# Prompt attention of a two-layer decoder step: the order of the gate's multiplications by 1/sum against the evictions of score pieces

## The chip, the cores and the metric

The kernel runs on one core of a Trainium2 chip. A core has four engines that compute, each with its own queue of instructions that it runs in order: TensorE (PE in the profile; PEld is its loading of the stationary operand), VectorE (DVE), ScalarE (ACT) and GpSimd (POOL). SyncE (SP) issues transfers. Engines wait for each other by semaphores. TensorE writes into PSUM, eight banks of 2 KB in each of 128 partitions; VectorE and ScalarE bring results from there into SBUF. The metric is the device time of one execution, in microseconds; smaller is better.

## The reference, cut to what matters

One step of a two-layer decoder: an mLSTM layer, then a layer of attention with learned forgetting, each followed by a SwiGLU block, for a prompt of 1024 tokens behind 16 meta tokens and for 64 sampled tokens. The change lies in the attention of the prompt. With `q`, `k` already normalised and `c` the running sum of the log-forget values, that is

```python
s = jnp.einsum('bhqd,bkhd->bhqk', qi, k)          # 16 heads of 64
s = s + ci[..., None] - ckT[:, :, None, :]
s = jnp.where(pos_k[None, :] <= pi[:, None], s, -jnp.inf)
p = jax.nn.softmax(s, axis=-1)
o = jnp.einsum('bhqk,bkhd->bqhd', p, v)
...
return (o * jax.nn.sigmoid(og)) @ w_out
```

The kernel takes the division by the softmax's sum out of `p`: it multiplies `o * sigmoid(og)` by 1/sum afterwards, which is the same number.

## The kernel before, in words

The sixteen heads are taken as eight pairs (`hp`); the two heads of a pair lie in the two halves of the partitions (`z` = 0, 1). The 1024 queries are eight blocks of 128 (`qb` = 1 to 8), and two blocks (`u` = 0, 1) make a group `g` of 256 queries. Groups are worked in the order 0, 3, 1, 2 (`QG`).

**Score pieces.** `scores` (L2571) makes the scores of one block piece by piece (`KSPLIT`: up to 512 keys in a piece, 14 pieces in a head pair). A piece is two PSUM tiles `sp`, one for each head; the pool holds three. TensorE fills both with six matmuls that alternate between them (L2596; the inputs are split into a high and a low half, so there are three products for each). VectorE then evicts z = 0 and z = 1, each with one or two instructions (L2600) that add the forget values or the mask and keep the running maximum, which is read out behind each (DVE_READ_ACCUMULATOR). After a block's last piece POOL computes the bias `nb` (L2613, L2614), and ScalarE takes the exponentials in place, with their sum (L2623).

**Units.** A group's probabilities are worked in units of two key blocks; the last unit of a group is its tail. `turn` (L2636) transposes the probabilities on TensorE into a tile `tp` of two PSUM banks (two such tiles), ScalarE copies them out (L2658); a tail has columns left in `tp`, at places 6 and 7 of each half. In a tail the last 16 keys go through places 6 and 7 of the second half and are copied by L2660; VectorE takes 1/sum (L2663), and POOL spreads it over 64 columns (`rx`, L2666). `prod` (L2668) multiplies the transposed probabilities with the values into the output tile `op` (one bank; L2683, L2687, L2691). In a tail it also ends the group:

- four *spreading transposes* (L2678) first turn `rx`, so that 1/sum lies over the queries: two into places 6 and 7 of the first half of `tp`, two into columns 256 to 383 of the output bank;
- behind the product, VectorE multiplies the gate `og` by the output (L2694, 256 columns) and then the result by the two halves of 1/sum (L2697 twice, 128 columns each), one from `tp`, one from the output bank;
- POOL splits the result into a high and a low half (L2705, L2706).

**The order** is written out by hand, for TensorE, VectorE, ScalarE and POOL alike (`manual_schedule`). The loop over units (L2748 on) emits: a score piece if one is due (`ahead`), the unit's `turn`, its exponentials, another score piece if one is due, then the `prod` of the unit before. Pieces run 9 ahead (`LEAD`) and come at 0.7 for each call; so the pattern is the same for each head pair, and in it every tail's `prod` stands right behind a score piece, except at the end, when pieces have run out.

Of the kernel before, what the change touches and what calls it, by code (L numbers as in the profile page):

```python
# [11 lines left out]
ALU = mybir.AluOpType  # L12
# [2443 lines left out]
def attend_prompt(self, ys, slots, both, w):  # L2456


    nc, tc = self.nc, self.tc
    with self.pool("ap", bufs=1) as sp, self.pool("ap2", bufs=2) as s2, self.pool("app", bufs=2, space=PSUM) as pp:  # L2460
# [107 lines left out]

        rows = {}

        def scores(hp, g):  # L2571
# [7 lines left out]
            for u in range(2):  # L2579
# [11 lines left out]
                for n in KSPLIT[qb]:  # L2591
                    ps = [pp.tile([P, 512], F32, name=f"sp{hp}_{qb}_{c}_{z}", tag="sp", bufs=3) for z in range(2)]
                    for y, (a, b) in enumerate(((qh, kh), (qh, kl), (ql, kh))):
                        for z in range(2):
                            r = slice(z * 64, z * 64 + 64)
                            nc.tensor.matmul(ps[z][:, :n], a[r, qs], b[r, at : at + n], start=(y == 0), stop=(y == 2))  # L2596
                    parts = [(0, n)] if at + n < nk else [(0, n - P), (n - P, n)]
                    for z in range(2):
                        for y, (o, e) in enumerate(parts):
                            nc.vector.tensor_tensor_reduce(  # L2600
                                out=ss[z, u][:, at + o : at + e], in0=ps[z][:, o:e],
                                in1=diag[x][:, z] if y else ncb[:, z, at + o : at + e], scale=1.0,
                                scalar=mx[:, z, c + y - 1 : c + y] if c + y else NEG, op0=ALU.add, op1=ALU.max,
                                accum_out=mx[:, z, c + y : c + y + 1])
# [13 lines left out]
        def exps(n):  # L2618

            for _ in range(n):  # L2620
                _, _, ss, u, nb, sm = todo_exp.pop(0)
                for z in range(2):
                    nc.scalar.activation(ss[z, u], ss[z, u], AF.Exp, bias=nb[:, z : z + 1],  # L2623
                                         accum_out=sm[:, u, z : z + 1])

        def units(hp, g):


            vr, og = vals[hp]
# [5 lines left out]
            for j0 in range(0, nf, 2):  # L2635
# [3 lines left out]
                def turn(j0=j0, tail=tail, hold=hold):  # L2639
# [19 lines left out]
                    if tail:  # L2659
# [6 lines left out]
                        nc.gpsimd.tensor_copy(rx, hold["r"].unsqueeze(3).broadcast_to([P, 2, 2, DH]))  # L2666

                def prod(j0=j0, tail=tail, hold=hold):  # L2668
                    th = hold["th"]
                    mm = nc.tensor.matmul  # L2670
                    if tail:


                        hold["rs"] = [hold["pt"][:, 0, 6:], po[:, 256:384].rearrange("p (u q) -> p u q", u=2)]
                        for u in range(2):
                            for h, x in enumerate(hold["rs"]):
                                r = slice(h * 64, h * 64 + 64)
                                mm(x[:, u], hold["rx"][r, u].rearrange("p z d -> p (z d)"), self.ident[r, r],  # L2678
                                   start=(h == 0 or j0 == 0), stop=True, is_transpose=True, skip_group_check=True)
                    ds = [slice(z * 64, z * 64 + 64) for z in range(2)]  # L2680
# [13 lines left out]
                    nc.vector.tensor_tensor(out=y, in0=po[:, :256], in1=y, op=ALU.mult)  # L2694
                    for h, x in enumerate(hold["rs"]):
                        yh = y.rearrange("p (u h q) -> p h u q", u=2, h=2)[:, h]
                        nc.vector.tensor_tensor(out=yh, in0=x, in1=yh, op=ALU.mult)  # L2697
                    c0 = T0 + 256 * g
# [9 lines left out]

                out.append((turn, prod))
            return out  # L2710
# [12 lines left out]
        with tc.manual_schedule(engines={E.PE, E.DVE, E.Activation, E.Pool}):  # L2723
# [10 lines left out]
            def ahead(slot):  # L2734

                nonlocal made
                while made < ns and made < LEAD + slot * ns / (2 * nu):
                    next(todo, None)
                    made += 1
                    if slot == 0:  # L2740
                        for _ in range(2):
                            next(gate, None)
                        exps(len(todo_exp) - 1)

            late = None
            slot = 0
            todo_exp = []
            for hp, g in groups:  # L2748
                us = None
                for k in range(g + 1):  # L2750
# [14 lines left out]
                    us[k][0]()  # L2765
                    exps(n)
                    ahead(slot + 1)
                    if late:
                        late()
                    late = us[k][1]  # L2770
                    slot += 2
# [7 lines left out]
                if (hp, g) in groups[4:6]:  # L2779
                    next(tile0)  # L2780
            late()
    return ws
# [34 lines left out]
```

## Time and profile before

| what | value |
|---|---|
| median of 3 runs | 2872.78 us (2870.52 to 2873.95) |
| the profiled execution's own time | 2874.75 us |
| its span in the profile | 2873.1 us |
| prompt attention within the span | about 1791 to 2024 us |
| granted TensorE clock, mean | 0.997 |
| output product's multiplication, L2694 | 32 times, median 421 ns |
| multiplication by 1/sum, L2697 | 64 times, 280 to 293 ns |
| spreading transposes, L2678 | 128 times, median 220 ns |

A row of the timeline gives the start within the span, the time taken, the engine, the line, the operation, the tiles (result, arrow, inputs), the shape and how many instructions are merged; in brackets the idle time of that engine just before, and what ended it by the profile. For TensorE the ends of matmuls are modelled, and they overlap: a row's time is not what the engine is held for. Waits are listed as "who <- for whom: total, times, longest". Releasers are inferred: of several semaphores the last is named.

### The profile page before, as it was taken

What the parts mean: (1) busy time and instruction counts of PE and PEld (TensorE: products, weight loads), DVE (VectorE), ACT (ScalarE), POOL (GpSimd) and SP (SyncE); (2) the same over time, 40 slices, a digit from 0 to 9 for tenths busy, and PEclk for the clock granted to TensorE, in tenths of its full rate; (3) what the DMA queues carried; (4) which work ended last, traced back from release to release, by engine and by line L of the source; (5) the groups of instructions that cost most, each with busy time, mean ns of one, the idle gap of its engine ahead of it and who ended that gap; (6) DMA issues with size and microseconds to landing.
All of it is one profiled execution on the core that took longest, in us unless ns stands there. A gap on an engine that the chain in (4) does not pass through costs nothing.

```text
span 2873.1 us, 53648 instructions
## 1 busy us (share of the span) xinstructions
PE 2795.3 (97%) x20485; PEld 2674.7 (93%) x20485; DVE 1726.0 (60%) x3478; ACT 1310.9 (46%) x2622; POOL 1017.8 (35%) x1495
## 2 busy tenths in 40 slices
PE   7999989999999999999999999999999999999999
PEld 7998979999999999999999888677999999999999
DVE  6044555887777655553345444776478777765553
ACT  6122464444444434443444444777344444443432
POOL 3022333075556311115352102454307655531210
PEclk9999999999999999999999999999999999999999
DMA  7057656122222275544453676442413222237652
GB/s 214 16 144 170 164 159 182 49 88 78 79 84 78 98 264 197 203 150 136 139 174 123 238 279 220 143 148 85 158 48 94 75 75 84 78 98 255 219 184 101
DMA packets 312443, 400.19 MB, mean 139 GB/s; under 512 B 28142, under 2 KB 235050, under 8 KB 311162
## 3 DMA queue, kind: packets, MB, share of 16 engines
q1 hardware_dynamic: 277234, 277.79, 30.4%
q0 software_dynamic: 33728, 118.38, 12.6%
q8 instruction: 161, 2.64, 0.4%
q14 instruction: 96, 0.79, 0.1%
q10 hardware_dynamic: 1224, 0.60, 0.1%
HBM read 299.92 MB, written 96.77 MB: 138 GB/s over the span
## 4 chain that ended last, share of the span: by engine, by line
PE 69%; DVE 10%; issue 4%; ACT 3%; DMA 2%; POOL 1%; DVEq 0%; ACTq 0%; POOLq 0%; SPq 0%
PE m L1505 23%; PE dps L266 6%; PE dps L268 6%; PE dps L267 6%; PE tmps L266 3%; PE tmps L267 3%; PE tmps L268 3%; DVE slot L339 2%; PE sp L2596 1%; DVE s L2600 1%; PE op L2683 1%; PE pops L266 1%; PE pops L267 1%; PE pops L268 1%; PE bps L266 1%
## 5 line engine op out<-in xcount | busy, mean ns | idle before, releaser
L339 DVE TENSOR_TENSOR slot<-slot,slot 128x1024 fp32r<-128x1024 f32 (+3 forms) x263 | 266.5, 1016 | 133.9 <-ACT slot L338 125.4
L338 ACT CAST slot<-slot 128x1024 fp32r<-128x1024 f32 (+3 forms) x263 | 206.7, 788 | 236.3 <-PE dps L267 90.1
L1505 PE MATMUL m<-x1h,slot 128*128 128x384 f32 x640 | 178.3, 338 | 3.1 <-DVE ns L1481 1.5
L1505 PE MATMUL m<-x0h,slot 128*128 128x336 f32 x640 | 167.0, 316 | 0.0
L413 POOL TENSOR_TENSOR ns<-ns,nq 128x384 f32<-128x384 f32 (+1 forms) x59 | 63.8, 1081 | 210.9 <-ACT nq L411 209.7
L1505 PE MATMUL m<-x2h,slot 128*128 128x384 f32 x480 | 135.8, 337 | 0.0
L1612 POOL DMA_DIRECT2D hr<-hT x60 | 32.5, 542 | 281.6 <-DVE T_2l L339 68.8
L108 POOL TENSOR_TENSOR slot<-vA 128x256 f32<-128x256 f32 x80 | 74.9, 946 | 151.2 <-DMA vA<-in_w_gate_up 147.5
L108 POOL TENSOR_TENSOR slot<-Ht 128x256 f32<-128x256 f32 x80 | 74.9, 946 | 150.9 <-DMA Ht<-in_w_gate_up 147.2
L339 DVE TENSOR_TENSOR slot<-Ht,slot 128x256 fp32r<-128x256 f32 (+3 forms) x101 | 84.9, 842 | 63.6 <-ACT slot L338 63.6
L339 DVE TENSOR_TENSOR slot<-vA,slot 128x256 fp32r<-128x256 f32 (+3 forms) x101 | 85.5, 849 | 62.2 <-ACT slot L338 62.2
L1505 PEld LDWEIGHTS m<-x1h,slot 128*128 128x128 f32 x640 | 117.1, 188 | 4.4 <-DVE ns L1481 2.1
L1505 PEld LDWEIGHTS m<-x0h,slot 128*128 128x128 f32 x640 | 113.3, 188 | 0.0
L1505 PE MATMUL m<-x1l,slot 128*128 128x384 f32 x320 | 107.8, 337 | 0.0
L1505 PE MATMUL m<-x0l,slot 128*128 128x336 f32 x320 | 101.0, 316 | 0.0
L1505 PE MATMUL m<-T_2h,slot 128*128 128x384 f32 x320 | 96.8, 343 | 3.0 <-ACT Ht L1511 0.9
L2623 ACT ACTIVATE s<-s,nb 128x272 f32<-128x272 f32 (+7 forms) x126 | 98.9, 786 | 0.1
L2658 ACT COPY th<-tp 128x768 f32<-128x768 f32 (+1 forms) x80 | 73.4, 919 | 55.3 <-PE tp L2650 32.6
L1505 PE MATMUL m<-T_4h,slot 128*128 128x384 f32 x320 | 95.3, 338 | 0.0
L108 POOL TENSOR_TENSOR Ht<-Ht 128x512 f32<-128x512 f32 (+1 forms) x60 | 84.5, 1408 | 28.4 <-DVE wl1l L339 28.4
L108 POOL TENSOR_TENSOR vA<-vA 128x512 f32<-128x512 f32 (+1 forms) x60 | 84.4, 1408 | 27.5 <-DVE wl0l L339 27.5
L2029 DVE TENSOR_REDUCE ss<-sqb 128x4 f32<-128x256 f32 (+1 forms) x72 | 30.2, 419 | 102.8 <-ACT sqb L2028 102.0
(843 smaller groups left out, 10286.8 us busy)
## 6 DMA issues: line engine op xcount, KB each, us to landing
slot<-in_w_down SPq DMA_DIRECT2D x88, 512.0 KB, 4.4
wr<-in_w_down SPq DMA_DIRECT2D x42, 512.0 KB, 4.7
wraw<-in_w_in_a SPq DMA_DIRECT2D x40, 512.0 KB, 4.0
vA<-in_w_gate_up SPq DMA_DIRECT2D x40, 512.0 KB, 3.9
Ht<-in_w_gate_up SPq DMA_DIRECT2D x40, 512.0 KB, 4.1
hr<-hT POOLq DMA_DIRECT2D x46, 384.0 KB, 5.5
kp<-in_cache_k SPq DMA_DIRECT2D x32, 512.0 KB, 5.6
vp<-in_cache_v SPq DMA_DIRECT2D x32, 512.0 KB, 6.3
```

The source lines that it names most:

```text
L108: self.net.nc.gpsimd.tensor_tensor(out=o, in0=a, in1=b, op=op)
L266: mm(ps, sh, mh, start=first, stop=False)
L267: mm(ps, sh, ml, start=False, stop=False)
L268: mm(ps, sl, mh, start=False, stop=last)
L338: self.nc.scalar.copy(hi, src)
L339: self.nc.vector.tensor_tensor(out=lo, in0=src, in1=hi.bitcast(F32), op=ALU.subtract)
L413: (nc.vector if x >= late else nc.gpsimd).tensor_tensor(out=s, in0=s, in1=sq, op=ALU.add)
L1505: nc.tensor.matmul(u.b[b][:, :n], w[p][:, k], x[q][:, k], start=new and k == i == 0, stop=k == 1 and i == 2, skip_group_check=True)
L1612: nc.gpsimd.dma_start(hraw[j], hT[t][:, 2 * c : 2 * c + 2])
L2029: nc.vector.tensor_reduce(out=ss[:m, i, :], in_=sq[:m].rearrange("p (h d) -> p h d", d=DH), op=ALU.add, axis=AX.X)
L2623: nc.scalar.activation(ss[z, u], ss[z, u], AF.Exp, bias=nb[:, z : z + 1], accum_out=sm[:, u, z : z + 1])
L2658: nc.scalar.copy(th.rearrange("p x z (u h q) -> p h (x z u) q", h=2, q=64)[:, :, :n], pt[:, :, :n])
```

## The change

The part of `prod` that multiplies by 1/sum becomes two functions of its own. `spread` issues the four spreading transposes, now all into places 6 and 7 of the two halves of `tp`. `scale` issues the two multiplications of `og` by 1/sum, before `og` is multiplied by the output. The loop hands the pair to the next score piece: `scores` calls `spread` behind the piece's six matmuls, and `scale` between the eviction of z = 0 and that of z = 1. If no piece comes, `flush` calls both just ahead of `prod`. The multiplication by the output comes last.

```diff
--- before.py
+++ after.py
@@ -2567,6 +2567,7 @@
                                         in1=mask.unsqueeze(1).broadcast_to([P, 2, P]), op=ALU.add)
 
         rows = {}
+        between = []
 
         def scores(hp, g):
 
@@ -2595,7 +2596,12 @@
                             r = slice(z * 64, z * 64 + 64)
                             nc.tensor.matmul(ps[z][:, :n], a[r, qs], b[r, at : at + n], start=(y == 0), stop=(y == 2))
                     parts = [(0, n)] if at + n < nk else [(0, n - P), (n - P, n)]
+                    spread, scale = between.pop() if between else (None, None)
+                    if spread:
+                        spread()
                     for z in range(2):
+                        if z and scale:
+                            scale()
                         for y, (o, e) in enumerate(parts):
                             nc.vector.tensor_tensor_reduce(
                                 out=ss[z, u][:, at + o : at + e], in0=ps[z][:, o:e],
@@ -2665,18 +2671,22 @@
                             [P, 2, 2, DH], F32, name=f"rx{hp}_{g}", tag="rx")
                         nc.gpsimd.tensor_copy(rx, hold["r"].unsqueeze(3).broadcast_to([P, 2, 2, DH]))
 
+                def spread(j0=j0, hold=hold):
+                    hold["rs"] = [hold["pt"][:, h, 6:] for h in range(2)]
+                    for u in range(2):
+                        for h, x in enumerate(hold["rs"]):
+                            r = slice(h * 64, h * 64 + 64)
+                            nc.tensor.matmul(x[:, u], hold["rx"][r, u].rearrange("p z d -> p (z d)"), self.ident[r, r],
+                                             start=True, stop=True, is_transpose=True, skip_group_check=True)
+
+                def scale(hold=hold):
+                    for h, x in enumerate(hold["rs"]):
+                        yh = og[g].rearrange("p (u h q) -> p h u q", u=2, h=2)[:, h]
+                        nc.vector.tensor_tensor(out=yh, in0=x, in1=yh, op=ALU.mult)
+
                 def prod(j0=j0, tail=tail, hold=hold):
                     th = hold["th"]
                     mm = nc.tensor.matmul
-                    if tail:
-
-
-                        hold["rs"] = [hold["pt"][:, 0, 6:], po[:, 256:384].rearrange("p (u q) -> p u q", u=2)]
-                        for u in range(2):
-                            for h, x in enumerate(hold["rs"]):
-                                r = slice(h * 64, h * 64 + 64)
-                                mm(x[:, u], hold["rx"][r, u].rearrange("p z d -> p (z d)"), self.ident[r, r],
-                                   start=(h == 0 or j0 == 0), stop=True, is_transpose=True, skip_group_check=True)
                     ds = [slice(z * 64, z * 64 + 64) for z in range(2)]
                     for x in range(1 if tail else 2):
                         for z in range(2):
@@ -2692,9 +2702,6 @@
                                start=False, stop=(u == 1))
                     y = og[g]
                     nc.vector.tensor_tensor(out=y, in0=po[:, :256], in1=y, op=ALU.mult)
-                    for h, x in enumerate(hold["rs"]):
-                        yh = y.rearrange("p (u h q) -> p h u q", u=2, h=2)[:, h]
-                        nc.vector.tensor_tensor(out=yh, in0=x, in1=yh, op=ALU.mult)
                     c0 = T0 + 256 * g
                     for t, (t0, t1) in enumerate(TS):
                         a, b = max(c0, t0), min(c0 + 256, t1)
@@ -2706,7 +2713,7 @@
                             nc.gpsimd.tensor_tensor(out=xl[:, hp, xs], in0=ya, in1=xh[:, hp, xs].bitcast(F32),
                                                     op=ALU.subtract)
 
-                out.append((turn, prod))
+                out.append((turn, prod, (spread, scale) if tail else None))
             return out
 
         groups = [(hp, g) for hp in range(8) for g in QG]
@@ -2741,6 +2748,12 @@
                         for _ in range(2):
                             next(gate, None)
                         exps(len(todo_exp) - 1)
+
+            def flush():
+                for pair in between:
+                    for f in pair:
+                        f()
+                between.clear()
 
             late = None
             slot = 0
@@ -2764,10 +2777,13 @@
                         n = max(n - m, 0)
                     us[k][0]()
                     exps(n)
+                    if late and late[2]:
+                        between.append(late[2])
                     ahead(slot + 1)
                     if late:
-                        late()
-                    late = us[k][1]
+                        flush()
+                        late[1]()
+                    late = us[k]
                     slot += 2
                     if g == QG[1] and k == 2 and hp < 7:
                         load_v(hp + 1, nc.sync)
@@ -2778,7 +2794,9 @@
                         wo_split(k)
                 if (hp, g) in groups[4:6]:
                     next(tile0)
-            late()
+            for f in late[2]:
+                f()
+            late[1]()
     return ws
```

On VectorE, at the tail of group 2 (`og_2`), with the last piece of block 4 (`s_4_0`, `s_4_1`: z = 0 and 1) and the first of block 5, the order before was:

```order
L2600 ISA s_4_0_19364,mx_4_19366<-sp_4_1_0_19408,nd_4_19138,mx_4_19366 128x128
...
L2600 ISA s_4_1_19365,mx_4_19366<-sp_4_1_1_19409,ncb_18561,mx_4_19366 128x128
...
L2600 ISA s_4_1_19365,mx_4_19366<-sp_4_1_1_19409,nd_4_19138,mx_4_19366 128x128
...
L2694 TENSOR_TENSOR og_2_18599<-op_2_19228,og_2_18599 128x256
L2697 TENSOR_TENSOR og_2_18599<-tp_2_4_19336,og_2_18599 128x2x64
L2697 TENSOR_TENSOR og_2_18599<-op_2_19228,og_2_18599 128x2x64
L2600 ISA s_5_0_19446,mx_5_19448<-sp_5_0_0_19449,ncb_18561 128x400
```

and on the same engine at the same place after it:

```order
L2606 ISA s_4_0_19364,mx_4_19366<-sp_4_1_0_19408,nd_4_19138,mx_4_19366 128x128
...
L2685 TENSOR_TENSOR og_2_18599<-tp_2_4_19336,og_2_18599 128x2x64 x2
L2606 ISA s_4_1_19365,mx_4_19366<-sp_4_1_1_19409,ncb_18561,mx_4_19366 128x128
...
L2606 ISA s_4_1_19365,mx_4_19366<-sp_4_1_1_19409,nd_4_19138,mx_4_19366 128x128
...
L2704 TENSOR_TENSOR og_2_18599<-op_2_19228,og_2_18599 128x256
L2606 ISA s_5_0_19446,mx_5_19448<-sp_5_0_0_19449,ncb_18561 128x400
```

Both multiplications by 1/sum (now L2685) moved from behind the output product's to between the two evictions, and both read `tp`; L2704 is the former L2694.

On TensorE, at the tail of group 3 with the first piece of block 7, the order before was:

```order
L2596 MATMUL sp_7_0_0_20282<-kh_19702,ql_19704 128x512
L2596 MATMUL sp_7_0_1_20283<-kh_19702,ql_19704 128x512
L2678 MATMUL tp_3_6_20197<-ident,rx_3_20219 128x64
L2678 MATMUL op_3_20032<-ident,rx_3_20219 128x64
L2678 MATMUL tp_3_6_20197<-ident,rx_3_20219 128x64
L2678 MATMUL op_3_20032<-ident,rx_3_20219 128x64
L2683 MATMUL op_3_20032<-th_3_6_20198,vr_19591 64x256 x2
L2687 MATMUL op_3_20032<-th_3_6_20198,vr_19591 64x128 x2
L2691 MATMUL op_3_20032<-tail_18551,vr_19591 64x32 x4
L2596 MATMUL sp_7_1_0_20309<-kh_19702,qh_19701 128x400
```

and after it:

```order
L2597 MATMUL sp_7_0_0_20282<-kh_19702,ql_19704 128x512
L2597 MATMUL sp_7_0_1_20283<-kh_19702,ql_19704 128x512
L2679 MATMUL tp_3_6_20197<-ident,rx_3_20219 128x64 x4
L2693 MATMUL op_3_20032<-th_3_6_20198,vr_19591 64x256 x2
L2697 MATMUL op_3_20032<-th_3_6_20198,vr_19591 64x128 x2
L2701 MATMUL op_3_20032<-tail_18551,vr_19591 64x32 x4
L2597 MATMUL sp_7_1_0_20309<-kh_19702,qh_19701 128x400
```

Nothing moved on TensorE; only the target of two of the four spreading transposes (now L2679) is another.

## The prediction

> **What bounds the kernel now.** The shares by engine and the windows come first: they say which engine limits the stage that the change touches. The profiled run took 2874.75 us, 2.0 above the median of the runs shown (2872.78) and 1.7 above its own span; what is won or lost below is taken off the median.
>
> ```profile
> span 2873.1 us, 53648 instructions
> ...
> PE 2795.3 (97%) x20485; PEld 2674.7 (93%) x20485; DVE 1726.0 (60%) x3478; ACT 1310.9 (46%) x2622; POOL 1017.8 (35%) x1495
> ...
> 1791.00:2024.00 233.00, 216.54 (x3062) 162.32 (x3062) 162.58 (x783) 176.44 (x362) 111.82 (x291) 0.99 0.40 130
> 2023.00:2060.00 37.00, 37.00 (x234) 36.81 (x233) 15.00 (x22) 10.01 (x16) 14.64 (x20) 1.00 0.69 226
> ```
>
> Prompt attention lies in 1791 to 2024 us. The columns of the window are length, then busy time of PE, PEld, DVE, ACT, POOL. TensorE is busy 216.5 of 233 us, so all its visible idle time is 16.5 us, and the change cannot win more than about that. Behind the stage TensorE is busy without a gap (37.00 of 37.00), so what the stage wins is kept. Next come the waits of the stage (us in total, times, longest).
>
> ```profile
> DVE s L2600 <- PE sp L2596: 29.7, 29, 2.4
> ...
> DVE og L2694 <- PE op L2691: 8.1, 3, 4.6
> PE sp L2596 <- DVE mx L2600: 7.2, 17, 0.9
> ...
> PE tp L2650 <- DVE og L2697: 4.0, 7, 0.6
> ```
>
> VectorE waited for the output product only 3 times in 32 tails: elsewhere, when it reaches the product's multiplication, the product is there already. So VectorE idles ahead of a piece's first eviction (29.7 us), not between evictions and gate. TensorE in turn waits for evictions (7.2) and, once per head pair, for the gate multiplication that frees a transposes' tile (4.0). The timeline shows how these meet. The order of one head pair comes back every 28.9 us (1913.86 to 1942.75 under C), with the same four tails. I call them A (group 3, with the first piece of block 7), B (group 1, second piece of block 8), C (group 2, last piece of block 4 of the next pair), D (group 0, last piece of block 5).
>
> Place A:
>
> ```profile
> 1954.18 0.22 PE L2678 MATMUL tp<-ident,rx 64*128 64x64 f32 x1
> ...
> 1954.43 0.69 DVE L2600 CUSTOM_DVE_ANT_0 s<-sp,slot 128x512 f32<-128x512 f32 x1 [1.06 <-PE op L2678]
> ...
> 1955.05 0.69 DVE L2600 CUSTOM_DVE_ANT_0 s<-sp,slot 128x512 f32<-128x512 f32 x1
> ...
> 1955.66 0.42 DVE L2694 TENSOR_TENSOR og<-op,og 128x256 f32<-128x256 f32 x1
> ...
> 1956.18 0.29 DVE L2697 TENSOR_TENSOR og<-tp,og 128x128 f32<-128x128 f32 x1
> 1956.39 0.28 DVE L2697 TENSOR_TENSOR og<-op,og 128x128 f32<-128x128 f32 x1
> ...
> 1956.58 0.49 DVE L2600 CUSTOM_DVE_ANT_0 s<-sp,slot,mx 128x272 f32<-128x272 f32 x1
> ...
> 1957.73 0.76 PE L2596 MATMUL sp<-slot,slot 64*128 64x384 f32 x5 [0.52 <-DVE mx L2600]
> ```
>
> From 1954.43 VectorE runs without a gap: eviction z=0, eviction z=1, output product, two multiplications by 1/sum, next piece. At 1957.73 TensorE has waited 0.52 us for that next piece's z=0. The spreading transposes were done at 1954.40, long before the first eviction ended.
>
> Place C, with the row of the head pair before it first:
>
> ```profile
> 1913.86 0.71 PE L2650 MATMUL tp<-ident,s 64*128 64x64 f32 x16 [0.58 <-DVE og L2697]
> ...
> 1940.34 0.35 DVE L2600 CUSTOM_DVE_ANT_0 s<-sp,ncb,mx 128x128 f32<-128x128 f32 x1 [1.50 <-PE sp L2596]
> ...
> 1941.12 0.35 DVE L2600 CUSTOM_DVE_ANT_0 s<-sp,ncb,mx 128x128 f32<-128x128 f32 x1
> ...
> 1941.78 0.42 DVE L2694 TENSOR_TENSOR og<-op,og 128x256 f32<-128x256 f32 x1
> ...
> 1942.31 0.29 DVE L2697 TENSOR_TENSOR og<-tp,og 128x128 f32<-128x128 f32 x1
> ...
> 1942.71 0.56 DVE L2600 CUSTOM_DVE_ANT_0 s<-sp,ncb 128x400 f32<-128x400 f32 x1
> ...
> 1942.75 0.71 PE L2650 MATMUL tp<-ident,s 64*128 64x64 f32 x16 [0.58 <-DVE og L2697]
> ...
> 1943.20 0.08 DVE L2600 DVE_READ_ACCUMULATOR2_ANT mx<- 128x1 f32 x1
> ...
> 1943.24 0.49 PE L2596 MATMUL sp<-kh,qh 64*128 64x256 f32 x2
> ```
>
> Here the transposes of the next unit wait 0.58 us for the first multiplication by 1/sum. Places B and D, the waits for the output bank:
>
> ```profile
> 1933.02 0.42 DVE L2694 TENSOR_TENSOR og<-op,og 128x256 f32<-128x256 f32 x1
> ...
> 1933.39 0.66 PE L2650 MATMUL tp<-ident,s 64*128 64x64 f32 x16
> ...
> 1933.76 0.28 DVE L2697 TENSOR_TENSOR og<-op,og 128x128 f32<-128x128 f32 x1
> ...
> 1934.19 0.44 PE L2683 MATMUL op<-th,vr 128*64 128x256 f32 x2
> ...
> 1945.33 0.42 DVE L2694 TENSOR_TENSOR og<-op,og 128x256 f32<-128x256 f32 x1
> ...
> 1946.07 0.28 DVE L2697 TENSOR_TENSOR og<-op,og 128x128 f32<-128x128 f32 x1
> ...
> 1946.49 1.08 PE L2683 MATMUL op<-th,vr 128*64 128x256 f32 x8 [0.18 <-PE sp L2596]
> ```
>
> The next group's first product writes the bank that the second multiplication still reads: that one ends at 1933.76 + 0.28 = 1934.04 and at 1946.35, and the product starts 0.15 and 0.14 later. The row names "PE sp", but the order of starts says it is this release.
>
> **The change, part by part.** *Nothing is added or removed.* The four spreading transposes and the three multiplications of each of the 32 tails stay, with their sizes; on TensorE they keep their places behind the score matmuls and ahead of the product. Cost 0 there. The transposes now write only the probabilities' tile; they waited already for the copy of that tile's tail (ScalarE) and for the spread sums (POOL), and still do.
>
> *The burst on VectorE.* Before, from the output product to the next piece: 0.52 (1955.66 to 1956.18) + 0.21 + 0.19 = 0.92; at C 1941.78 to 1942.71, 0.93. The 0.52 holds a gap of 0.10 behind the product, because the multiplication reads what it wrote. Afterwards the two multiplications stand ahead of z=1 (0.21 + 0.19, they follow each other without a wait), and the product is followed by an eviction that does not need it. That pair is not in the trace. Bounds: at most the 0.52 as now, at least 0.34, which is 0.42 less the 0.08 by which the two multiplications overlap (0.29 long, 0.21 apart). I take 0.34 or 0.35, since a follower that reads nothing of it is nearest to that pair. The burst then takes 0.40 + 0.35 = 0.75, **0.17 shorter**. The bound from above is 0.
>
> *A* is then 0.17 shorter, 7 times (in the last head pair no piece is left at the last three tails): the wait of 0.52 shrinks to 0.35. It does not go, because VectorE has the same work between its first eviction and the next piece.
>
> *C.* The tile is free after the second multiplication, 1941.12 + 0.21 + 0.28 = 1941.61, so the wait of 0.58 goes. What is late next: the score piece behind those transposes needs the z=0 eviction that begins at 1942.71, read out at 1943.20. Before, the transposes' wait covered that; afterwards the read-out comes at 1943.03, and TensorE, there at about 1942.7, stands again until about 1943.16. The wait changes its name, and 0.17 is won, 7 times.
>
> *B and D.* The output bank is freed by the end of the product, which starts 0.40 later than now: at B 1933.02 + 0.40 + 0.42 = 1933.84 in place of 1934.04, 0.19 to 0.20 earlier. At B the transposes end at 1934.05 and products elsewhere start just as such a row ends, so TensorE can use it. 0.19 x 7 at B. D has a score piece in the first head pair too, 0.19 x 8.
>
> *The end.* In the last head pair nothing stands between:
>
> ```profile
> 2016.93 0.71 PE L2650 MATMUL tp<-ident,s 64*128 64x64 f32 x16
> 2017.05 0.43 DVE L2694 TENSOR_TENSOR og<-op,og 128x256 f32<-128x256 f32 x1 [0.25 <-PE op L2691]
> ...
> 2017.71 0.28 DVE L2697 TENSOR_TENSOR og<-op,og 128x128 f32<-128x128 f32 x1
> ...
> 2018.14 1.08 PE L2683 MATMUL op<-th,vr 128*64 128x256 f32 x8 [0.50 <-DVE r L2663]
> ```
>
> With both multiplications done beforehand the bank is free at 2017.05 + 0.43 = 2017.48, the transposes end at 2017.64: 0.5 is won, once.
>
> *What the move puts at risk.* The z=1 eviction ends 0.40 later in the tails. Behind it wait the bias on POOL, then the exponentials; at D:
>
> ```profile
> 1945.84 0.19 POOL L2614 TENSOR_TENSOR nb<-nb,cqP 128x2 f32<-128x2 f32 x1
> ...
> 1946.80 0.84 ACT L2623 ACTIVATE s<-s,nb 128x656 f32<-128x656 f32 x1
> ```
>
> The bias is there 0.77 before it is used, so 0.40 fits: 0. The piece two further on needs that buffer (at C from about 1942.4, wanted at 1942.7): 0.
>
> Sum: 7 x 0.17 + 7 x 0.19 + 7 x 0.17 + 8 x 0.19 + 0.5 = 1.2 + 1.3 + 1.2 + 1.5 + 0.5 = **5.7 us**, so 2872.8 - 5.7 = 2867.1. These waits lie one behind the other on the way TensorE, VectorE, TensorE, so they add.
>
> **Rivals.** *The gap stays whoever follows.* If the 0.52 behind the product stands with any follower, A and C win nothing; B, D and the end stay: 15 x 0.19 + 0.5 = 3.4, so 2869.4. The row for it is the 0.10 itself; against it, the two multiplications that start 0.21 apart although each lasts 0.28 or more. [...]
>
> *The waits go altogether.* If VectorE found time for the multiplications where it idles now, the waits of A, C and D would vanish: 7 x (0.52 + 0.58 + 0.19) + 8 x 0.18 + 0.5 = 11.0, so 2861.8. For it speaks the idle 1.06 and 1.50 ahead of the first evictions; against it, that the multiplications stand behind that first eviction, not in the gap.
>
> *It does not reach the end.* ScalarE is busy 176 of 233 us, and if its copies end the same waits, nothing is won: 2872.8. Against it: no row of A to D names ScalarE.
>
> *Slower.* If VectorE restarts with the 0.10 gap at each of the three new joints (first eviction to multiplication, multiplication to second eviction, that to product), the burst grows by 0.30 - 0.17 = 0.13 at A and C, and the release at B and D comes 0.30 - 0.19 = 0.11 later: 14 x 0.13 + 15 x 0.11 - 0.5 = 3.0, so 2875.8; with the wait for the transposes paid in each tail too (0.1 x 29) 2878.7. It decides from 0.6 us for the two multiplications in place of 0.40. Against it, the product now starts with the read-out of the eviction ahead of it, without a gap.
>
> **How the numbers follow.** 0.2% is 5.7 us, about what a measurement of this kernel can tell from no change. The forecast has 0.52 and lies on that bound; I put 0.33 of it beyond, as no small gain (a wait instruction less on TensorE in some tails) is in the sum, and 0.19 within. The staying gap has 0.13 and the unreached end 0.07, both within. The vanishing waits have 0.16, all faster. The slower case has 0.12: 0.07 beyond, 0.05 within. So faster 0.49, same 0.44, slower 0.07. The range runs from 2861.5 (waits gone) to 2874.5 (nothing won and the spread of the runs, 1.2 above the median); outside lie most of the slower case and some of the fastest, about 0.15. The likeliest case by itself has 2865 to 2869.
>
> **What would show it.** Right: the wait of the transposes for the gate (4.0, 7 times) is gone and the wait of score matmuls for evictions has grown at C to about 0.4 and fallen to about 0.35 at A; the output product is followed by an eviction 0.34 to 0.35 later; the head pair's period falls from 28.9 to about 28.2. Wrong: a gap at the new joints, the product still 0.52 ahead of its follower, an exponential that waits for the bias, or waits at A that vanish.

## The result: 7.75 us less, most of it found in prompt attention

The changed kernel takes 2862.77 us (median of 11 runs, 2856.89 to 2866.77), the kernel before 2870.52 us (median of 11 runs, 2866.90 to 2873.95). The ratio is 0.9977 with an interval of 0.9969 to 0.9985, that is 4.3 to 8.9 us faster. A second measurement gave 0.9978 (0.9969 to 0.9987). The forecast was 2867.1, or 5.7 less than before.

The profiled spans differ by more than the medians. Here is the head of the page of the changed kernel:

```profile
span 2855.2 us, 53625 instructions
...
PE 2790.4 (98%) x20485; PEld 2671.0 (94%) x20485; DVE 1724.8 (60%) x3478; ACT 1311.8 (46%) x2622; POOL 1018.3 (36%) x1495
```

Of the 17.9 us between the spans, 9.9 lie ahead of prompt attention: its first score matmul starts at 1773.41 before and at 1763.56 after, and nothing was changed ahead of it. So the stage has to be measured by itself. I take it from one instruction to another that both kernels have: the last output-gate product ahead of the first transposes (1791.18 before) to the first product of the output projection (2024.65 before). The columns are those of the window rows in the prediction. The kernel before, its first profile:

```profile
1791.18:2024.65 233.47, 217.01 (x3066) 162.79 (x3066) 163.05 (x783) 176.26 (x362) 112.29 (x291) 0.99 0.40 130
```

and a second one, taken later (before_again, below):

```profile
1784.50:2016.36 231.86, 215.49 (x3065) 162.05 (x3065) 162.95 (x782) 176.37 (x362) 112.30 (x291) 1.00 0.40 131
```

The changed kernel, its first profile:

```profile
1781.14:2006.41 225.27, 215.03 (x3066) 161.86 (x3065) 160.08 (x784) 176.92 (x362) 112.35 (x292) 1.00 0.41 134
```

and a second one (after_again, below):

```profile
1787.17:2012.42 225.25, 215.02 (x3065) 161.85 (x3065) 160.08 (x784) 176.93 (x362) 111.94 (x292) 1.00 0.40 134
```

The stage is 225.27 and 225.25 us long, before 233.47 and 231.86. The 1.6 between the two profiles of the kernel before is no work: it is TensorE's clock, in the first profile (the seventh number, PEclk):

```profile
1840.00:1842.00 2.00, 1.40 (x8) 0.92 (x9) 1.43 (x10) 0.74 (x2) 1.22 (x5) 0.67 0.57 209
1842.00:1844.00 2.00, 2.00 (x12) 0.86 (x14) 0.87 (x4) 0.00 (x0) 0.98 (x2) 0.50 0.18 58
```

So the change is worth 231.86 - 225.25 = **6.6 us** in the stage at full clock. It comes from TensorE's idle time, 231.86 - 215.49 = 16.4 before and 225.25 - 215.02 = 10.2 after; VectorE's busy time fell from 163.0 to 160.1: the same operations follow each other more closely.

The waits of the stage (us in total, times, longest):

```profile
DVE s L2606 <- PE sp L2597: 26.8, 30, 1.7
...
PE sp L2597 <- DVE mx L2606: 7.7, 23, 0.9
...
DVE s L2606 <- POOL nb L2620: 7.4, 15, 0.7
...
DVE og L2704 <- PE op L2701: 0.9, 2, 0.5
```

The wait of the transposes for the gate multiplication (4.0, 7 times) has no row any more. The score matmuls' wait for evictions has grown in number from 17 to 23 and in sum from 7.2 to 7.7. Place A:

```profile
1938.85 0.69 DVE L2606 CUSTOM_DVE_ANT_0 s<-sp,slot 128x512 f32<-128x512 f32 x1 [1.05 <-PE tp L2679]
...
1939.47 0.48 DVE L2685 TENSOR_TENSOR og<-tp,og 128x128 f32<-128x128 f32 x2
1939.87 0.68 DVE L2606 CUSTOM_DVE_ANT_0 s<-sp,slot 128x512 f32<-128x512 f32 x1
...
1940.47 0.42 DVE L2704 TENSOR_TENSOR og<-op,og 128x256 f32<-128x256 f32 x1
1940.81 0.49 DVE L2606 CUSTOM_DVE_ANT_0 s<-sp,slot,mx 128x272 f32<-128x272 f32 x1
...
1941.96 0.76 PE L2597 MATMUL sp<-slot,slot 64*128 64x384 f32 x5 [0.32 <-DVE mx L2606]
```

From the first eviction to the next piece it takes 1940.81 - 1938.85 = 1.96 us in place of 2.15. The multiplications cost 0.40 (1939.47 to 1939.87) and stand there without a gap on either side; the product is followed 0.34 later. TensorE waits 0.32 in place of 0.52. Place C, with the same transposes one head pair earlier:

```profile
1898.83 0.65 PE L2656 MATMUL tp<-ident,s 64*128 64x64 f32 x16
...
1926.87 0.66 PE L2656 MATMUL tp<-ident,s 64*128 64x64 f32 x16
...
1927.04 0.42 DVE L2704 TENSOR_TENSOR og<-op,og 128x256 f32<-128x256 f32 x1
...
1927.38 0.57 DVE L2606 CUSTOM_DVE_ANT_0 s<-sp,ncb 128x400 f32<-128x400 f32 x1
...
1928.00 0.38 PE L2597 MATMUL sp<-kh,qh 64*128 64x256 f32 x1 [0.32 <-DVE mx L2606]
```

The transposes no longer wait. The score piece behind them now waits 0.32 for the eviction that begins at 1927.38. The period of a head pair is 1926.87 - 1898.83 = **28.04 us** (28.89 before). Places B and D:

```profile
1918.45 0.42 DVE L2704 TENSOR_TENSOR og<-op,og 128x256 f32<-128x256 f32 x1
1918.47 0.66 PE L2656 MATMUL tp<-ident,s 64*128 64x64 f32 x16
...
1919.06 0.65 PE L2693 MATMUL op<-th,vr 128*64 128x256 f32 x4
...
1930.39 0.42 DVE L2704 TENSOR_TENSOR og<-op,og 128x256 f32<-128x256 f32 x1
...
1930.89 0.20 POOL L2620 TENSOR_TENSOR nb<-nb,cqP 128x2 f32<-128x2 f32 x1
...
1930.92 0.87 PE L2693 MATMUL op<-th,vr 128*64 128x256 f32 x6
...
1931.39 0.85 ACT L2629 ACTIVATE s<-s,nb 128x656 f32<-128x656 f32 x1
```

Both next products start right behind what TensorE did before them (no idle time in TensorE's rows). At D the product's weight load still names VectorE's product, with 0.26 of idle time, but that is no loss: behind A's next piece (1942.65) a product's load stands 0.25 too, and names nobody. The bias on POOL comes later than before, but still 0.30 before the exponential uses it (1930.89 + 0.20 to 1931.39). VectorE itself now waits for the bias at D: the eviction behind the product starts 0.74 behind it, not 0.34, and such waits for POOL have grown from 5.1 us, 8 times, to 7.4, 15 times. By the starts of the matmuls behind D, TensorE loses nothing by it.

### The profile page after: what moved, and what is told of

Same layout as the page of the kernel before. It is cut to its first block, busy times and chain, and to the rows that moved or that the text cites. A ratio compares the mean times of both kernels' runs of the same rounds, so it can differ in the third digit from the quotient of the medians.

```text
span 2855.2 us, 53625 instructions
## 1 busy us (share of the span) xinstructions
PE 2790.4 (98%) x20485; PEld 2671.0 (94%) x20485; DVE 1724.8 (60%) x3478; ACT 1311.8 (46%) x2622; POOL 1018.3 (36%) x1495
## 4 chain that ended last, share of the span: by engine, by line
PE 71%; DVE 9%; issue 4%; ACT 3%; DMA 2%; POOL 1%; DVEq 0%; ACTq 0%; SPq 0%; POOLq 0%
PE m L1505 24%; PE dps L266 6%; PE dps L268 6%; PE dps L267 6%; PE tmps L266 3%; PE tmps L268 3%; PE tmps L267 3%; PE sp L2597 2%; DVE slot L339 2%; PE pops L268 1%; PE pops L266 1%; PE pops L267 1%; PE op L2693 1%; PE bps L266 1%; DVE s L2606 1%
```

## The experiments

Theory, *the dependent gap*: a VectorE instruction that reads what the instruction right ahead of it wrote starts 0.10 behind that one's end, some 0.18 later than an instruction that doesn't read it (0.52 behind the product's start in place of 0.34); the move takes this gap out, and what leaves VectorE's burst behind a piece's scores is won at A and C, while the earlier release of the output bank is won at B and D. The rivals: that the place of the halves alone, or "product last" alone, does it, that the gap stays whoever follows, or that VectorE's time counts for nothing. The period is taken from the starts of C's transposes, the stage as above.

| kernel | median us | before, same chip | ratio (interval) | stage us | period us |
|---|---|---|---|---|---|
| changed | 2862.77 | 2870.52 | 0.9977 (0.9969 to 0.9985) | 225.27 | 28.04 |
| place_only | 2866.84 | 2871.10 | 0.9985 (0.9976 to 0.9994) | 228.77 | 28.52 |
| behind_both | 2866.67 | 2871.10 | 0.9988 (0.9979 to 0.9997) | 229.38 | 28.61 |
| free_follower | 2861.69 | 2871.10 | 0.9966 (0.9954 to 0.9978) | 225.44 | 28.13 |
| early_scale | 2856.74 | 2871.10 | 0.9953 (0.9939 to 0.9966) | 223.32 | 27.53 |
| half_in_op | 2896.31 | 2870.89 | 1.0090 (1.0075 to 1.0106) | 261.53 | 32.47 |
| scale_twice | 2872.76 | 2870.89 | 1.0009 (1.0000 to 1.0018) | 235.14 | 29.44 |
| before_again | 2866.39 | 2868.77 | one run | 231.86 | 28.88 |
| after_again | 2862.42 | 2868.77 | 0.9978 (0.9969 to 0.9987) | 225.25 | 28.05 |
| early_again | 2858.31 | 2868.77 | 0.9969 (0.9958 to 0.9981) | 221.86 | 27.53 |

**Both halves in the probabilities' tile, order as before (place_only).** Against the changed kernel:

```diff
                 def prod(j0=j0, tail=tail, hold=hold):
                     th = hold["th"]
                     mm = nc.tensor.matmul
+                    if tail:
+                        spread()
...
                     nc.vector.tensor_tensor(out=y, in0=po[:, :256], in1=y, op=ALU.mult)
+                    scale()
...
-                    if late and late[2]:
-                        between.append(late[2])
```

> One part alone: both halves of 1/sum in the probabilities' tile, but spread and multiplied where they were (behind the output product). The period is that of a head pair, from one C's transposes to the next: 28.89 us in the kernel before, 28.04 in the changed one. Theory 'dependent gap': a VectorE instruction that reads what the one right ahead of it wrote starts 0.10 later (0.52 behind the product in place of about 0.34), and each 0.01 of VectorE's burst counts at A and C. Here the gap stays, so A is unchanged. B and D win what they won (0.21 and 0.24), because the output bank is free at the end of the product. C loses 0.20, because the tile is freed by the second multiplication in place of the first. Period 28.64; with 0.4 at the end of the stage some 2.3 us below the kernel before, about 2868.2. Rival 'the place of the halves is what counts': period 28.04, about 2862.8.

Measured: period 28.52. The gap is there, and A waits as before. The timeline of VectorE at A:

```profile
1948.54 0.42 DVE L2706 TENSOR_TENSOR og<-op,og 128x256 f32<-128x256 f32 x1
1949.06 0.49 DVE L2685 TENSOR_TENSOR og<-tp,og 128x128 f32<-128x128 f32 x2
```

B and D won 0.22 and 0.24. C's transposes waited 0.77 in place of 0.58, as expected, but the score piece behind them waited less, and only 0.10 of the 0.20 was lost. So the place of the halves alone earns B and D, less what it costs at C; it is not what wins A.

**Multiplications behind both evictions, product last (behind_both).**

```diff
                     for z in range(2):
-                        if z and scale:
-                            scale()
                         for y, (o, e) in enumerate(parts):
                             nc.vector.tensor_tensor_reduce(...
+                    if scale:
+                        scale()
```

> The changed kernel with the two multiplications by 1/sum behind both evictions, right ahead of the output product, which stays last. Theory 'dependent gap': now the product reads what the multiplication right ahead of it wrote, so the 0.10 comes back there (0.38 from the second multiplication to the product in place of 0.19). The burst is 0.21 + 0.38 + 0.34 = 0.93 as in the kernel before, and the output bank is freed at the old time: A, B, C and D win nothing; the end of the stage keeps its 0.5. Period 28.89, about 2870.0. Rival 'product last is enough, the place between the evictions is nothing': period 28.04, about 2862.8.

Measured: period 28.61, between the two. A's burst in the timeline:

```profile
1948.87 0.48 DVE L2685 TENSOR_TENSOR og<-tp,og 128x128 f32<-128x128 f32 x2
1949.46 0.42 DVE L2704 TENSOR_TENSOR og<-op,og 128x256 f32<-128x256 f32 x1
1949.80 0.49 DVE L2604 CUSTOM_DVE_ANT_0 s<-sp,slot,mx 128x272 f32<-128x272 f32 x1
```

From the multiplications to the next piece it is 0.93, just as expected: the pair takes 0.59 to the product (0.40 where an eviction follows), so the gap is back, now ahead of the product, and A waits 0.52 as before. So "product last" alone does not do it; the eviction between the multiplications and the product is what fills the gap. I missed B and D, which won 0.16 and 0.09. The timeline at D:

```profile
1938.92 0.42 DVE L2704 TENSOR_TENSOR og<-op,og 128x256 f32<-128x256 f32 x1
...
1939.40 0.20 PEld L2693 LDWEIGHTS op<-th,vr 128*64 128x64 f32 x4 [0.41 <-DVE og L2704]
```

The weight load starts 0.06 behind the product's end (1938.92 + 0.42). Before, it started 0.11 behind the end of the multiplication (1946.07 + 0.28, load at 1946.46), and the first matmul another 0.03 behind its load (1946.49); here the two start together. What is gone is an instruction of 51 ns on TensorE's queue of weight loads that does nothing but wait. Before, the next product had two semaphores to wait for, VectorE's and TensorE's own, and the wait for VectorE's was an instruction by itself at each of the 15 places B and D. The profile of the line in the kernel before, and of the same line in behind_both (how many, shortest, median and longest in ns, first and last start in us):

```profile
L2683 PEldq EVENT_SEMAPHORE  x17: 51/51/51, 1798.4 to 2018.0; - x17
```

```profile
L2693 PEldq EVENT_SEMAPHORE  x8: 51/51/51, 1820.7 to 2004.4; - x8
```

None of the 8 that are left stands at B or D. At D the load now waits by itself, and TensorE starts 0.09 sooner behind its release: that is D's 0.09. place_only has none at these places either, so it comes with 1/sum leaving the output bank. The rest at B, some 0.06, is VectorE's: before, its product stood some 0.06 behind the read-out of z = 1, for TensorE's output product; here the multiplications fill that time.

**The same order as place_only, but a follower that does not depend (free_follower).** The output lacks the factor 1/sum.

```diff
                     for h, x in enumerate(hold["rs"]):
-                        yh = og[g].rearrange("p (u h q) -> p h u q", u=2, h=2)[:, h]
-                        nc.vector.tensor_tensor(out=yh, in0=x, in1=yh, op=ALU.mult)
+                        nc.vector.tensor_tensor(out=spare[:, h], in0=x,
+                                                in1=self.ident.rearrange("p (u q) -> p u q", u=2), op=ALU.mult)
```

> As place_only, but the two multiplications read the identity in place of the gate and write a tile of their own, so that they don't depend on the product ahead of them: the output is left without its factor 1/sum. Durations and order are the same. Theory 'dependent gap': product to multiplication falls from 0.52 to 0.33 or 0.34, A and C win 0.18 each against place_only: period 28.28, about 2865.7. Rival 'the gap stays whoever follows' (or belongs to the change of the source from one tile to the other): 0.52 stays, period 28.64, about 2868.2.

The timeline of VectorE at A, from the product on:

```profile
1946.43 0.42 DVE L2707 TENSOR_TENSOR og<-op,og 128x256 f32<-128x256 f32 x1
1946.77 0.48 DVE L2685 TENSOR_TENSOR spare<-tp,ident 128x128 f32<-128x128 f32 x2
1947.17 0.49 DVE L2607 CUSTOM_DVE_ANT_0 s<-sp,slot,mx 128x272 f32<-128x272 f32 x1
```

Measured: 0.34 in place of 0.52, with instructions of the same kind and size in the same order; only the gate's tile is replaced, by the identity as an input and by a tile of its own as the output. A waits 0.31, the period falls from 28.52 to 28.13. So the gap goes with the dependence and does not stay whoever follows.

The 0.18 has two parts, though. The dependent multiplication waits for two semaphores, VectorE's and ScalarE's, and here too the first of these waits is an instruction by itself (21 ns; 30 for the 32 tails of the kernel before, 1 in free_follower). At two tails of the kernel before it waits for VectorE's alone:

```profile
L2697 DVEq EVENT_SEMAPHORE  x30: 21/21/21, 1797.8 to 2023.1; - x30
```

```profile
1838.67 0.41 DVE L2694 TENSOR_TENSOR og<-op,og 128x256 f32<-128x256 f32 x1
1839.12 0.29 DVE L2697 TENSOR_TENSOR og<-tp,og 128x128 f32<-128x128 f32 x1
```

There it starts 0.45 behind the product's start (0.46 at the other, 2017.05), at the 30 others 0.52 or 0.53. So waiting for what was just written cost 0.11 to 0.12 behind this product (0.45 or 0.46 in place of 0.34), and the second semaphore 0.07 more. The first of the two tails is an A, and the changed kernel won 0.13 there, where it won 0.19 or 0.20 at most others.

**Half of 1/sum left in the output bank (half_in_op).**

```diff
-                    hold["rs"] = [hold["pt"][:, h, 6:] for h in range(2)]
+                    hold["rs"] = [hold["pt"][:, 0, 6:], po[:, 256:384].rearrange("p (u q) -> p u q", u=2)]
```

> The other part alone: the multiplications by 1/sum between the evictions and the product last, as in the changed kernel, but the second half of 1/sum stays in the output bank, as in the kernel before. Theory: the output product, which writes that bank, then waits until the multiplication between the evictions has read it. In the changed kernel the product starts with the z=0 eviction; here it would start 0.11 behind the second multiplication: at A (eviction 0.62, then 0.48) 1.2 later, at B (0.54 and 0.48) 1.1, at C and D (0.78 and 0.48) some 1.3. Less the waits of 0.30 at A and 0.31 at C, which that covers, some 4.2 us per head pair: period 32.2, some 30 us above the changed kernel, about 2893. Rival 'the place of the halves is a matter of neatness, the order earns the gain': period 28.04, about 2862.8.

The timeline at C, the second multiplication and the product that waits for it:

```profile
1918.51 0.28 DVE L2685 TENSOR_TENSOR og<-op,og 128x128 f32<-128x128 f32 x1
...
1918.84 0.65 PE L2693 MATMUL op<-th,vr 128*64 128x256 f32 x4 [1.24 <-DVE og L2685]
```

Measured: period 32.47, 25.4 us slower than before. The product waits 1.24 at this place (C) for the multiplication that reads its bank. So the order wins only together with the place: with half of 1/sum in the output bank, the same order costs almost four times what the two together win.

**The multiplications twice (scale_twice).**

```diff
                         nc.vector.tensor_tensor(out=yh, in0=x, in1=yh, op=ALU.mult)
+                    for h, x in enumerate(hold["rs"]):
+                        nc.vector.tensor_tensor(out=spare[:, h], in0=x,
+                                                in1=self.ident.rearrange("p (u q) -> p u q", u=2), op=ALU.mult)
```

> The changed kernel, and behind the two multiplications by 1/sum, still between the evictions, two more of the same shape (the same halves times the identity, onto a tile that nothing reads): 0.40 more in VectorE's burst of each tail. Theory 'each 0.01 of the burst counts where a wait hangs on it': A and C 0.40 later, B 0.27 and D 0.35 later (the output bank is freed 0.40 later, of which some was spare). Period 28.04 + 1.42 = 29.46, 10.3 us above the changed kernel, about 2873. Rival 'VectorE has room (busy 69% of the stage), 0.40 is swallowed': period 28.04, about 2862.8.

Measured: period 29.44, 10.0 us above the changed kernel by the medians and 9.9 by the stage. The four places lost 0.40 (A), 0.26 (B), 0.39 (C) and 0.34 (D). The waits in this kernel's stage:

```profile
PE sp L2598 <- DVE mx L2607: 11.3, 23, 0.9
...
PE op L2697 <- DVE og L2708: 3.9, 16, 0.4
```

VectorE is busy 172 of 235 us, and still what is added behind a piece's scores is paid in full at A and C; at B 0.14 of the 0.40 was spare and at D 0.06.

**Spread and multiplied ahead of the evictions (early_scale).**

```diff
+                    spread, scale = between.pop() if between else (None, None)
+                    if spread:
+                        spread()
                     for y, (a, b) in enumerate(((qh, kh), (qh, kl), (ql, kh))):
...
-                    spread, scale = between.pop() if between else (None, None)
-                    if spread:
-                        spread()
                     for z in range(2):
-                        if z and scale:
+                        if z == 0 and scale:
                             scale()
```

> The changed kernel with the spreading transposes ahead of the six score matmuls and the two multiplications ahead of the z=0 eviction, in the time in which VectorE stands idle (1.05 at A, 1.22 at B, 1.50 at C). Theory 'VectorE's burst behind the scores sets the waits': 0.40 leaves the burst, so the waits of score matmuls for evictions that the changed kernel still has at A (0.30) and C (0.31) go; B and D have no wait left and win nothing. Period 28.04 - 0.61 = 27.43, 7 x 0.61 = 4.3 less, about 2858.5. Rival: the spreading transposes, that much earlier, stand for POOL's spread sums or ScalarE's copy of the tail, and the score matmuls behind them with them; or the waits are set by something other than the burst: period 28.04 or more, 2862.8 or more.

The timeline at A, from the multiplications to the next piece:

```profile
1939.50 0.49 DVE L2685 TENSOR_TENSOR og<-tp,og 128x128 f32<-128x128 f32 x2 [0.38 <-ACT s L2629]
...
1940.30 0.69 DVE L2606 CUSTOM_DVE_ANT_0 s<-sp,slot 128x512 f32<-128x512 f32 x1 [0.31 <-PE sp L2600]
...
1941.09 0.81 PE L2600 MATMUL sp<-slot,slot 64*128 64x400 f32 x6
...
1941.53 0.42 DVE L2704 TENSOR_TENSOR og<-op,og 128x256 f32<-128x256 f32 x1
...
1941.94 0.50 DVE L2606 CUSTOM_DVE_ANT_0 s<-sp,slot,mx 128x272 f32<-128x272 f32 x1
```

Measured: period 27.53 (expected 27.43). The multiplications now lie ahead of the scores' end, the wait at C is gone, and 0.12 of A's wait is left: the product's follower starts 0.41 behind it, not 0.34, because the scores that it evicts end only at 1941.90 (1941.09 + 0.81): VectorE has caught up with TensorE. This kernel beats both. Its first ratio looked like more than its period gives, so it was run again, together with the two others.

**Second profiles (before_again, after_again, early_again).**

> The kernel before, profiled a second time. In the first profile TensorE's granted clock falls to 0.50 for some 3 us inside the stage (0.67 in 1840 to 1842 us, 0.50 in 1842 to 1844), and that costs 1.4 us which the profiles of the changed kernel, place_only, behind_both, free_follower and scale_twice don't show. Theory 'chance': the dip comes in some executions of any kernel; the stage (from the last output-gate product ahead of the first transposes to the first product of the output projection, 233.47 us) is then 233.5 or 232.0 in this profile, whichever. Rival 'the order of the kernel before draws it': the dip stands at the same instruction again. The period is 28.89 by both.

> The changed kernel, profiled and timed a second time, next to early_again. Theory: period 28.04; stage 225.3, or 226.7 if the dip of the clock falls into this execution; 7 us below the kernel before (about 0.9976).

> The kernel of early_scale, profiled and timed a second time, next to after_again. Its first profile had the dip of the clock. Theory 'chance': period 27.53 again, stage 223.3 with the dip or 221.9 without; 7 x 0.51 = 3.6 us below the changed kernel, about 0.9963 of the kernel before (the first measurement, 0.9953, then stands high in its gain). Rival: the first gain was right and there is more than the period to it: 14 us below the kernel before.

The periods came back to within 0.01. The dip of the clock did not come again in the kernel before, nor in early_again, where it had stood in the first profile at the same product (1.97 us long in both, 1.08 without). So the order of the kernel does not fix it, and its 1.6 us are left out of what the change is worth; whether one order sees it more often than another, two profiles of each can't say. early_again gave 0.9969, nearer to the 0.9963 that the period asks for than the first 0.9953; the stage says 231.86 - 221.86 = 10.0 us below the kernel before and 225.25 - 221.86 = 3.4 below the changed one.

## Why the prediction was right, and where its sizes were off

- *What bounds the stage.* Right: TensorE's idle time shrank where VectorE releases it, at the four places named. One more wait of a score matmul for an eviction went, 0.35 once, in the seventh head pair (1980.49 in the kernel before). It also went in behind_both, free_follower and scale_twice, and not in place_only; why, no run here shows. That ScalarE would end the same waits (nothing reaches the end) is refuted: the stage is 6.6 shorter.
- *The burst on VectorE.* Right in size: 0.40 for the multiplications, 0.34 behind the product, and free_follower shows that the gap goes with the dependence. That it stays with any follower is refuted by the same run. The reason was only half right: of the 0.10 behind the product's end, which the forecast put down to reading what was written, 0.03 is that, and 0.07 is the second semaphore. That the sum held all the same is in part luck: the change takes both away together.
- *A.* Forecast 0.17, measured 0.19 to 0.20 in four of the seven pairs (0.52 to 0.32). In the first it was 0.39, because the two multiplications stood 0.39 apart there before, in place of 0.21, and in the second 0.13, where the gap was the shorter one. In the fourth pair nothing was won, in both profiles: transposes ahead of it took 0.17 longer. Why, no run here shows.
- *C.* Right in kind: the wait for the gate went, and a wait for the eviction of 5_0 took its place. It is 0.32, not 0.4; won were 0.18 (0.74 gone, 0.56 back).
- *B and D.* Too small: 0.19 forecast, 0.21 and 0.24 measured. TensorE no longer waits for the bank there at all, so the win is the whole of what it stood, the start behind the release included (0.15 and 0.14 behind the multiplication's end by the rows), which I had assumed would go on. Of that start, 0.09 was the separate wait (behind_both), the small gain that the forecast named and left out of its sum. In the first head pair the 0.24 at D was not kept: the next product then waits 0.25 longer for ScalarE's copy.
- *The end.* Forecast 0.5, measured 0.6 as the sum of a larger gain and a new wait. TensorE arrives there 1.1 earlier (a wait of 1.07 for ScalarE's copy is gone) and wins 0.4 at the output bank, but pays 0.3 at ScalarE's next copy and 0.65 at POOL's spread sums, for which it waited 0.45 before. The rows of the changed kernel:

```profile
1997.05 0.17 DVE L2669 RECIPROCAL r<-sm 128x4 f32<-128x4 f32 x1
1997.36 0.40 POOL L2672 COPY rx<-r 128x256 f32<-128x256 f32 x1 [1.69 <-DVE r L2669]
...
1997.81 0.34 PE L2679 MATMUL tp<-ident,rx 64*128 64x64 f32 x4 [1.10 <-POOL rx L2672]
```

ScalarE and POOL are what is late next there, and this I had not named.

- *What was at risk.* The bias came 0.30 before its use, TensorE met no buffer that was late, and no gap stood at the three new joints; where VectorE does wait, behind the product at D for the bias, it cost TensorE nothing. The slower case was refuted in its mechanism. scale_twice shows what it would have cost.
- *The sum.* Forecast 5.7; the places give 7 x 0.24 (D) + 7 x 0.21 (B) + 7 x 0.18 (C) + 1.3 (A, all seven) + 0.6 + 0.35 (the wait in the seventh pair) = 6.7, the stage 6.6, the medians 7.75 with an interval that holds all of these. The terms that were mis-sized are the release at B and D, 0.3 us together, and the 0.35 is in no term.
- *The rival that I gave 0.16*, in which the waits go altogether, was a good kernel but not this one: early_scale does it, and wins 10 of the 11.0 worked out for it.

## What to carry to other kernels

On an engine that runs its instructions in order, look not only at how many there are between two waits, but at which reads the one right ahead of it: putting an independent instruction between the two took 0.18 us out of each burst here with no work removed. Count the semaphores that an instruction waits for as well: a second one cost 0.07 on VectorE, behind the product that the instruction reads, and 0.09 on TensorE, at D. Better still is to move work from behind the event that starts the burst to ahead of it, where the engine stands idle: the same two multiplications, 0.40 us, cost nothing there (early_scale: a period of 27.53 in place of 28.04). Before comparing two profiled spans, cut out the stage between two instructions that both kernels have and look at the granted clock in it; here more than half of the difference between the spans was not the change.

## What was not expected of the hardware

- TensorE's granted clock fell to 0.50 for 3.4 us in the stage (0.67, 0.50 and 0.98 in three windows of 2 us of the kernel before, from 1840), in 3 of 11 profiles (the first of the kernel before, the first of early_scale, half_in_op), each time in the first full head pair. Ahead of it TensorE had stood idle for part of the time: busy 1.40 of 2.00 us in the window in which it begins in the kernel before, 0.93 in the window ahead in early_scale, and in half_in_op 1.05 in the window ahead and 0.49 in the one in which it begins. A product of 1.08 us then took 1.97, and the stage some 1.5 us more. Outside the stage it comes too: between 216 and 236 us the mean clock is 0.91 in the first profile of the kernel before and in that of the changed kernel. The same kernel shows the fall in the stage in one execution and not in the next (0.99 and 1.00 mean clock of the stage, before and before_again, early_scale and early_again); what draws it, no run here shows.
- A second semaphore to wait for cost time of its own at two places: one of the two waits was an instruction by itself there (51 ns on TensorE, 21 ns on VectorE). On TensorE the next group's weight load began 0.06 us behind the end of VectorE's instruction with one semaphore to wait for (behind_both) and 0.11 with two (the kernel before); on VectorE a multiplication began 0.03 behind the product that it reads with one, and 0.10 with two (2 and 30 tails of the kernel before).
